# Layer 0's first modulation in four column chunks, the q projection summed with them, and q ahead of k/v for the later tiles

## The chip, the cores and the metric

The kernel runs on one core of one Trainium2 chip. A core has a matrix engine (TensorE; PE in the profile, its weight loads as PEld), a vector engine (VectorE, DVE), a scalar engine (ScalarE, ACT), GpSimd (POOL) and a sync engine (SP) that issues most transfers; 16 DMA engines move data between the chip's memory and the core's working memory. The metric is the device time of one execution in microseconds, the median of several runs.

## The reference

The reference is a diffusion backbone of two layers over 1024 latent tokens of width 1024 with a prefix of 256 context tokens. Only the entry of layer 0 matters here. From the condition vectors `c` (latent) and `c_ctx` (context) a modulation is computed, and tokens are scaled and shifted by its first two sixths; then one matrix gives the heads of two kinds of attention:

```python
m_lat = silu(c) @ ada_w[l] + ada_b[l]        # 6 x 1024 columns; m_ctx likewise from c_ctx
h_lat = x * (1 + m_lat[1]) + m_lat[0]        # h_ctx likewise
qa, ka, va, qb, kb, vb = split(h @ w_in, [512, 640, 768, 1280, 1792])   # 2304 columns
qa, ka = rms_norm(qa, q_gain), rms_norm(ka, k_gain)    # per head of 64 columns
qa, ka = apply_rope(qa, cos, sin), apply_rope(ka, cos, sin)   # latent tokens only
```

Attention, output projection, normalisation and a gated convolutional feed-forward follow, then layer 1. The other four sixths of `m_lat` and `m_ctx` are needed later.

## The kernel before, in words

Tokens are handled in ten tiles of 128: tiles 0 to 7 are latent, 8 and 9 are context. The function `l0_project` computes layer 0's projections. Products are made in three parts (`mm3`, L401 to L403): activations and weights are split into a high and a low half, and hi x hi, hi x lo and lo x hi are summed in PSUM, over eight blocks of 128 rows. A weight piece of 512 KB is loaded into a buffer of the ring `raw` (L125), and its halves are made by ACT (L112) and VectorE (L113).

The stages stand in this order on PE:

1. The head. `ada_first` loads the first 2048 columns of `ada_w[0]` as 16 tiles `wt` of 128 x 1024 (rows of 4 KB, L183) and multiplies `silu` of both condition vectors with them (L185). When all 16 are summed, four turns (L197) and a few small VectorE operations give the whole first modulation `mod0`. Meanwhile the rope table `rp`, then x of tiles 0 to 3 in two halves of 512 columns come in (L506).
2. `group(i, k)` turns one block of 128 columns of a group of four tiles (i = 0, 1; two context tiles for i = 2) on PE (L533), scales and shifts it on ACT into `sg` (L535) and makes the halves `hh` and `hl` (L542 to L545). Eight such groups of tiles 0 to 3 end the head. POOL makes the rope tables `tbq` and `tbk` from `rp` and the gains `gq` and `gk` (L555 to L563); VectorE scales `gq` first (L551).
3. k/v of tiles 0 to 3 (256 columns, weights `wk`), each with two groups of tiles 4 to 7 behind it; q of tiles 0 to 3 (512 columns, weights `wq`), each with two groups of the context behind it.
4. The generator `ada_items` is opened. It computes the other four sixths of layer 0's modulation on VectorE: loads `araw`, then `acc` sums (L231, L235), their halves (L322), a sum over partitions on PE (L325, L326), the bias (L330). Each `bg(n)` in the program takes up to n of its steps.
5. k/v of tiles 4 to 9 (with `bg(2)` at 8 and 9); q of tiles 4 to 9 with `bg(3)` each; v of the second attention, tiles 0 to 9 (weights `wv`), with `bg(3)` each. Behind v of tile 0 stand four turns (L145) with copies by VectorE (L147, `cc`) that bring the convolution's weights into columns.

A finished q or k tile is evacuated by `rms_rope`: ACT squares it (L584), VectorE sums per head (L586, `ss`) and makes the rotation's two products `rp` (L436, L446; for context tiles one product, L599), POOL makes the norm's factor (L589, L592), adds the products (L450) and scales (L605). `put_T` then turns the tile on PE (L471) and VectorE makes the low half `qst` (L459). This last part is put into the list `late` and runs three tiles later (`tok`).

Under `manual_pe` PE executes in the order in which the code is written; the order of the other engines is set by the framework's scheduler. Each engine executes its row strictly in order. Buffers come from pools with a fixed number of them: an allocation waits until the oldest buffer's readers are done. SP issues loads in order too, so a load that waits for its buffer holds up those behind it.

Of the kernel before, what the change touches and what calls it, by code (L numbers as in the profile page):

```python
# [12 lines left out]
ALU = mybir.AluOpType  # L13
# [24 lines left out]
class Kern:  # L38
# [93 lines left out]
    def cols_late(self, tp, ppool, rows, tag, pool=None, bufs=1):  # L132
# [10 lines left out]
        def make():  # L143
            ps = self.t(ppool, [128, 512], "small")
            nc.tensor.transpose(ps[:, :n], rt[:n, :], self.ident[:n, :n])  # L145
            ct = self.t(pool or self.cst, [128, n], tag)
            nc.vector.tensor_copy(ct, ps[:, :n])  # L147
            return ct
# [3 lines left out]
    def cols(self, tp, ppool, rows, tag, pool=None, bufs=1):  # L152
        return self.cols_late(tp, ppool, rows, tag, pool, bufs)()
# [8 lines left out]
    def ada_first(self, loads):  # L162

        nc, io = self.nc, self.io
        with ExitStack() as es:
            tp = es.enter_context(self.pool("p0"))
            ap = es.enter_context(self.pool("p0a"))
            wp = es.enter_context(self.pool("p0w", bufs=9))
            pp = es.enter_context(self.pool("p0s", bufs=1, space=PSUM))
            bias = self.row128(io["ada_b"][0, 0:2048])  # L170
            ct = self.cols(tp, pp, [io["c8"], io["cc8"], bias], "ccol")
            self.cs = self.t(self.cst, [128, 2, 8], "cs")
            nc.scalar.activation(
                self.cs, ct[:, :16].rearrange("p (v k) -> p v k", v=2), AF.Silu
            )
            w = io["ada_w"][0].rearrange("(k p) n -> p k n", p=128)
            ps = [self.t(pp, [128, 512], f"a{h}") for h in range(2)]
            for x in ps:
                nc.vector.memset(x[:, :256], 0.0)
            for k in range(KT):  # L180
                for h in range(2):
                    wt = self.t(wp, [128, 1024], "wt")
                    nc.sync.dma_start(wt, w[:, k, h * 1024 : (h + 1) * 1024])  # L183
                    for c in range(4):
                        nc.tensor.matmul(  # L185
                            ps[h][32 * c : 32 * c + 2, :256], self.cs[:, :, k],
                            wt[:, c * 256 : (c + 1) * 256], start=k == 0, stop=k == KT - 1,
                            tile_position=(0, 32 * c), skip_group_check=True,
                        )
            loads()  # L190
            ar = self.t(ap, [128, 2, 256], "ar")
            nc.scalar.copy(ar[:, 0], ps[0][:, :256])
            nc.vector.tensor_copy(ar[:, 1], ps[1][:, :256])
            pt = self.t(pp, [128, 512], "small")
            for j in range(4):
                s = slice(j % 2 * 128, j % 2 * 128 + 128)
                nc.tensor.transpose(  # L197
                    pt[:, j * 128 : (j + 1) * 128], ar[:, j // 2, s], self.ident
                )
            m0 = self.t(self.cst, [128, 2, 8, 2], "mod0")  # L200
            for h in range(2):
                nc.vector.tensor_add(
                    m0[:, h].rearrange("p (c b) v -> p c b v", b=2),
                    pt[:, h * 256 : (h + 1) * 256].rearrange(
                        "p (b c v) -> p c b v", b=2, c=4
                    )[:, :, :, :2],
                    ct[:, 16 + 8 * h : 24 + 8 * h].rearrange(
# [276 lines left out]
    def l0_project(self):  # L484
# [28 lines left out]
        with self.manual_pe():  # L513
            self.ada_first(first_loads)
# [2415 lines left out]
```

## Time and profile before

| | us |
|---|---|
| median of 3 runs (2925.42 to 2927.96) | 2925.8 |
| the profiled execution | 2927.96 |
| its span | 2926.1 |
| head, up to the first k/v product | 43.85 |
| first k/v product to the second v tile | 117.3 |
| the mean granted clock of TensorE over the span | 0.976 |

The busy time of an engine as a share of the span is an average over stages that have different limits. For this change the first 161 us count: a row of the windows view gives, for a stretch of the span, each engine's busy time, the clock that TensorE was granted (1.00 is full speed), the busy share of the DMA engines and the rate. A row of the timeline or of the chain of waits gives start, duration, engine, line and what is written from what; in the timeline, brackets hold the idle time before it and what ended that.

### The profile page before, as it was taken

What the parts mean: (1) busy time and instruction counts of PE and PEld (TensorE: products, weight loads), DVE (VectorE), ACT (ScalarE), POOL (GpSimd) and SP (SyncE); (2) the same over time, 40 slices, a digit from 0 to 9 for tenths busy, and PEclk for the clock granted to TensorE, in tenths of its full rate; (3) what the DMA queues carried; (4) which work ended last, traced back from release to release, by engine and by line L of the source; (5) the groups of instructions that cost most, each with busy time, mean ns of one, the idle gap of its engine ahead of it and who ended that gap; (6) DMA issues with size and microseconds to landing.
All of it is one profiled execution on the core that took longest, in us unless ns stands there. A gap on an engine that the chain in (4) does not pass through costs nothing.

```text
span 2926.1 us, 45178 instructions
## 1 busy us (share of the span) xinstructions
PE 2765.7 (95%) x16596; PEld 2254.8 (77%) x16596; DVE 2117.6 (72%) x3832; ACT 1383.0 (47%) x2597; POOL 691.5 (24%) x967
## 2 busy tenths in 40 slices
PE   6989999899999999999999987989998899999997
PEld 4877777777788988888888876866677688887886
DVE  4876366667588778888877656557766788888778
ACT  3221255567435655555553342257753545555541
POOL 2611143354451000000001013435544011111002
PEclk8999999999999999999999998989999999999999
DMA  8468711032567653333367526732244455555862
GB/s 261 141 188 275 229 39 41 11 128 94 160 161 241 207 169 107 119 107 114 117 236 272 163 83 195 226 106 64 65 132 146 126 172 164 176 171 201 325 219 93
DMA packets 370502, 456.87 MB, mean 156 GB/s; under 512 B 26137, under 2 KB 265017, under 8 KB 368745
## 3 DMA queue, kind: packets, MB, share of 16 engines
q1 hardware_dynamic: 342808, 369.40, 40.7%
q0 software_dynamic: 24576, 82.89, 8.2%
q8 instruction: 130, 2.13, 0.3%
q10 hardware_dynamic: 2896, 1.70, 0.2%
q14 instruction: 92, 0.75, 0.1%
HBM read 337.98 MB, written 115.93 MB: 155 GB/s over the span
## 4 chain that ended last, share of the span: by engine, by line
PE 68%; issue 10%; DVE 9%; DMA 6%; ACT 5%; POOL 1%; SPq 0%; ACTq 0%; DVEq 0%; POOLq 0%
PE q L1691 8%; PE x L1691 8%; PE y L1691 7%; PE S L762 4%; PE v L1691 4%; PE pv L907 3%; PE T L893 3%; PE dy L2354 3%; PE mm L401 2%; PE d L402 2%; PE d L403 2%; PE d L401 2%; PE mm L402 2%; PE mm L403 2%; PE dx L2354 2%
## 5 line engine op out<-in xcount | busy, mean ns | idle before, releaser
L786 POOL TENSOR_SCALAR P<-P,rin 128x640 f32<-128x640 f32 (+3 forms) x288 | 250.2, 873 | 347.3 <-DVE rin L785 324.0
L1665 DVE TENSOR_TENSOR w<-raw,w 128x512 fp32r<-128x512 f32 x308 | 207.3, 687 | 84.2 <-ACT w L1663 84.1
L112 ACT CAST w<-raw 128x512 fp32r<-128x512 f32 x315 | 183.3, 620 | 171.3 <-PE d L403 60.9
L113 DVE TENSOR_TENSOR w<-raw,w 128x512 fp32r<-128x512 f32 x299 | 194.2, 690 | 70.3 <-ACT w L112 68.2
L762 PE MATMUL S<-k,q 64*128 64x256 f32 (+2 forms) x1824 | 192.4, 338 | 16.9 <-DVE nm L2643 8.1
L783 ACT ACTIVATE P<-P,nm 128x641 f32<-128x641 f32 (+4 forms) x208 | 161.3, 777 | 83.0 <-DVE nm L2643 47.8
L1663 ACT CAST w<-raw 128x512 fp32r<-128x512 f32 x308 | 182.2, 621 | 13.8 <-DVE raw L1670 7.4
L762 PEld LDWEIGHTS S<-k,q 64*128 64x128 f32 x1824 | 136.1, 189 | 52.6 <-issue 17.8
L773 ACT COPY PT<-T 128x512 f32<-128x512 f32 (+1 forms) x250 | 134.0, 565 | 78.9 <-PE T L893 76.7
L907 PE MATMUL pv<-PT,v 128*64 128x128 f32 x2016 | 134.1, 281 | 16.3 <-ACT PT L773 14.1
L893 PE MATMUL T<-ident,P 128*128 128x128 f32 x1008 | 137.2, 283 | 7.9 <-POOL P L786 3.4
L907 PEld LDWEIGHTS pv<-PT,v 128*64 128x64 f32 x2016 | 109.5, 138 | 42.4 <-ACT PT L773 23.0
L401 PE MATMUL d<-w,w 128*128 128x512 f32 x352 | 138.0, 392 | 0.0
L403 PE MATMUL d<-w,w 128*128 128x512 f32 x352 | 137.7, 391 | 0.0
L402 PE MATMUL d<-w,w 128*128 128x512 f32 x352 | 137.6, 391 | 0.0
L785 DVE RECIPROCAL rin<-den 128x1 f32<-128x1 f32 x288 | 46.2, 162 | 121.0 <-ACT P L783 118.1
L893 PEld LDWEIGHTS T<-ident,P 128*128 128x128 f32 x1008 | 111.0, 143 | 28.5 <-issue 14.6
L771 DVE COPY PT<-T 128x512 f32<-128x512 f32 (+1 forms) x166 | 110.4, 666 | 30.7 <-PE T L893 20.6
L1691 PE MATMUL q<-T2h,w 128*128 128x512 f32 x352 | 117.7, 396 | 5.5 <-ACT q L1906 3.9
L1691 PE MATMUL q<-T3h,w 128*128 128x512 f32 x352 | 118.3, 397 | 4.0 <-DVE ug L2309 3.9
L2354 PE MATMUL dy<-w,w 128*128 128x512 f32 x528 | 120.8, 390 | 0.6 <-DVE w L113 0.6
L2643 DVE CUSTOM_DVE_ANT_0 P<-S,msk,snk 128x640 f32<-128x640 f32 (+1 forms) x128 | 103.7, 846 | 16.9 <-PE S L762 13.5
(417 smaller groups left out, 7802.2 us busy)
## 6 DMA issues: line engine op xcount, KB each, us to landing
raw<-in_up_dram SPq DMA_DIRECT2D x132, 512.0 KB
raw<-in_down_dram SPq DMA_DIRECT2D x59, 512.0 KB
raw<-g SPq DMA_DIRECT2D x44, 512.0 KB
raw<-G SPq DMA_DIRECT2D x38, 512.0 KB
araw<-in_ada_w_dram SPq DMA_DIRECT2D x32, 512.0 KB
raw<-in_w_in_dram SPq DMA_DIRECT2D x28, 512.0 KB
g<-cv POOLq DMA_DIRECT2D x22, 512.0 KB, 3.0
G<-go POOLq DMA_DIRECT2D x44, 256.0 KB, 2.7
```

What stands on the lines that cost most here:

```text
L112: nc.scalar.copy(hi, s)
L113: (lo_eng or nc.vector).tensor_sub(lo, s, f32(hi))
L401: nc.tensor.matmul(ps, lh, rh, start=first, stop=False)
L402: nc.tensor.matmul(ps, lh, rl, start=False, stop=False)
L403: nc.tensor.matmul(ps, ll, rh, start=False, stop=last)
L762: self.nc.tensor.matmul(outs[a], q[r, x, qs], k[r, y, ks], start=(i == 0), stop=(i == 2))
L786: nc.gpsimd.tensor_scalar(P[:, :n], P[:, :n], rin, 1.0, ALU.mult, ALU.mult)
L893: nc.tensor.transpose(ps[:, s * 128 : (s + 1) * 128], P[a][:, cols[i + x] : cols[i + x] + 128], self.ident,)
L907: nc.tensor.matmul(O[a * HD : (a + 1) * HD], v_of(a, vts[i + x]), pT[:, s * 128 : (s + 1) * 128], start=(i + x == 0), stop=(i + x == m - 1 ...
L1665: nc.vector.tensor_sub(half(i, 1), src[i], f32(half(i, 0)))
L1691: nc.tensor.matmul(ps, w[:, a, s], r[b][:, k], start=first and k + i == 0, stop=k == 3 and i == 2, skip_group_check=True,)
L2354: nc.tensor.matmul(banks[q][t], ga[i][:, a, c], wd[i][:, b], start=q < 2 and f + k == 0, stop=f == HF - 1 and k == 2, skip_group_check=True,)
```

## The change

The head is computed in four chunks j of columns. For each, four loads of 128 x 4 x 256 (pieces of 1 KB) bring the columns of shift and scale for two blocks k = 2j, 2j+1; `products(j, q)` multiplies half of a chunk (128 columns at a time), `turn_mod(j)` makes the two blocks' modulation, `turns(j)` turns the blocks of x, and `scaled` makes their halves. wq is loaded in four pieces of two blocks (`load_q`, `split_q`), and `part(j, t)` sums two of the eight blocks of q for tile t in a PSUM bank that is kept for each of tiles 0 to 3. So the sums of q begin when the first chunk is there. In this stretch the order is written by hand for PE, VectorE and ACT.

x is loaded in whole rows, in four buffers of 1024 columns in place of eight of 512. The rope table, gq, gk, wk and x of tiles 4 to 7 are loaded behind the head. Then q of tiles 0 to 3 is finished, k/v of tiles 0 to 3 follows with the groups of tiles 4 to 7, then q of tiles 4 to 9 with the context's groups, then k/v of tiles 4 to 9. `ada_items` is opened behind q of tile 7; `bg(3)` stands at q of tiles 8 and 9, `bg(2)` at k/v of tiles 4 to 9. `done` runs a waiting late part before it adds a new one.

```diff
-    def ada_first(self, loads):
+    def ada_first(self, tp, wp, pt, acc, m0):
...
+        def load(j):
+            for q in range(2):
+                for h in range(2):
+                    wt[j, q, h] = x = self.t(wp, [128, 4, 256], "wt")
+                    c0 = h * 1024 + j * 256
+                    nc.sync.dma_start(x, w[:, 4 * q : 4 * q + 4, c0 : c0 + 256])
+
+        def products(j, q):
+            s = slice(j % 2 * 128, j % 2 * 128 + 128)
+            for k in range(4 * q, 4 * q + 4):
+                for c in range(4):
+                    nc.tensor.matmul(
+                        acc[32 * c : 32 * c + 2, s], self.cs[:, :, k],
+                        wt[j, q, c // 2][:, k % 4, c % 2 * 128 : c % 2 * 128 + 128],
+                        start=k == 0, stop=k == KT - 1,
...
+            if q == 1:
+                ar[j] = self.t(tp, [128, 128], "ar", bufs=2)
+                nc.scalar.copy(ar[j], acc[:, s])
+
+        def turn(j):
+            ps = self.t(pt, [128, 4, 128], "tr")[:, 0]
+            nc.tensor.transpose(ps, ar[j], self.ident)
+            nc.vector.tensor_add(
+                m0[:, :, 2 * j : 2 * j + 2],
...
-        xp = ex.enter_context(self.pool("xp", bufs=8, side="right"))
+        xp = ex.enter_context(self.pool("xp", bufs=4, side="right"))
...
+        def load_q(j):
+            raws[j] = r = self.t(self.raw, [128, 2, 512], "raw")
...
+        def part(j, *ts):
+
+            for t in ts:
+                if j == 0:
+                    psq.append(self.t(pp, [128, 512], "mm"))
+                hi, lo, o = hT(t)
+                for k in (2 * j, 2 * j + 1):
+                    self.mm3(
+                        psq[t], hi[:, k, o : o + 128], lo[:, k, o : o + 128],
+                        *wq[k], k == 0, k == KT - 1,
+                    )
+
+        E = mybir.EngineType
+        engines = {E.PE, E.DVE, E.Activation}
+        with self.tc.manual_schedule(engines=engines), ExitStack() as e0:
...
+            def mod(j):
+                turn_mod(j)
+                for k in (2 * j, 2 * j + 1):
+                    scaled(0, k, trs.pop(k))
+
+            load_x(0)
+            load(0)
+            turns(0)
+            products(0, 0)
+            products(0, 1)
+            load_q(0)
+            load(1)
+            products(1, 0)
+            mod(0)
+            split_q(0)
+            load_q(1)
+            load(2)
+            products(1, 1)
+            part(0, 0, 1)
+            turns(1)
+            mod(1)
+            split_q(1)
+            part(0, 2, 3)
...
+            products(3, 0)
+            part(2, 0)
+            products(3, 1)
+            part(2, 1)
+            turns(3)
+            mod(3)
+            load_q(3)
+            split_q(3)
+            part(2, 2, 3)
...
+        def done(t, ps, ev):
             if len(late) > 3:
                 (late.pop(0) or int)()
+            late.append(ev(t, ps))
...
         with self.manual_pe():
-            load_x(1, 0)
-            load_x(1, 1)
-            wq = self.load_in(w, 0, 512)
+            load_x(1)
+            for t in range(4):
+                part(3, t)
+                done(t, psq[t], ev_qa)
             for t in range(4):
                 tok(t, wk, 256, ev_kva)
                 group(1, 2 * t)
                 group(1, 2 * t + 1)
-            load_x(2, 0)
-            load_x(2, 1)
-            for t in range(4):
+            load_x(2)
+            for t in range(4, NT):
                 tok(t, wq, 512, ev_qa)
-                group(2, 2 * t)
-                group(2, 2 * t + 1)
-            ex.close()
-            adap = es.enter_context(self.pool("adap", side="right"))
...
+                if t < 8:
+                    group(2, 2 * t - 8)
+                    group(2, 2 * t - 7)
+                if t == 7:
+                    ex.close()
+                    adap = es.enter_context(self.pool("adap", side="right"))
+                    ada = [
...
+                if t > 7:
+                    bg(3)
+            wv = self.load_in(w, 1792, 512)
             for t in range(4, NT):
                 tok(t, wk, 256, ev_kva)
-                if t > 7:
-                    bg(2)
-            wv = self.load_in(w, 1792, 512)
-            for t in range(4, NT):
-                tok(t, wq, 512, ev_qa)
-                bg(3)
+                bg(2)
```

In the rows that follow, a line number of the changed kernel is that of its own code (its `scaled` has L531 and L532 for the halves, its `rms_rope` L656 and L669, its rotation L432 and L442, `qst` L455, `acc` L227 and L231).

SP issues the loads. Before, at the end of x of tiles 0 to 3 (`x_254`, its last half row):

```order
L506 DMA x_254<-in_x_dram 128x1x512
L159 DMA gq_279<-in_qg_dram 128x64
L159 DMA gk_280<-in_kg_dram 128x64
L125 DMA raw_367<-in_w_in_dram 128x4x256
L125 DMA raw_375<-in_w_in_dram 128x4x256
L506 DMA x_394<-in_x_dram 128x1x512
```

After, from wq's last piece (`raw_494`) on; `raw_528` and `raw_536` are the two pieces of wk:

```order
L546 DMA raw_494<-in_w_in_dram 128x2x512
L620 DMA rp_114<-in_rope_dram 128x1024
L125 DMA raw_528<-in_w_in_dram 128x4x256
L159 DMA gq_524<-in_qg_dram 128x64
L159 DMA gk_525<-in_kg_dram 128x64
L501 DMA x_555<-in_x_dram 128x1x1024
L501 DMA x_557<-in_x_dram 128x1x1024
L501 DMA x_559<-in_x_dram 128x1x1024
L125 DMA raw_536<-in_w_in_dram 128x4x256
L501 DMA x_561<-in_x_dram 128x1x1024
```

The rope table, the gains and wk have moved behind the modulation's and q's weights, and x of tiles 4 to 7 comes in four whole tiles around wk's second piece.

VectorE in the head, before, from the end of `mod0` on:

```order
L211 TENSOR_SCALAR mod_79_264<-mod_79_264 128x16
L544 CAST hh_35_105<-sg_299 128x512
L545 TENSOR_TENSOR hl_36_106<-sg_299,hh_35_105 128x512
L544 CAST hh_35_105<-sg_317 128x512
L545 TENSOR_TENSOR hl_36_106<-sg_317,hh_35_105 128x512
L545 TENSOR_TENSOR hl_36_106<-sg_308,hh_35_105 128x512
L551 TENSOR_SCALAR gq_279<-gq_279 128x64
L544 CAST hh_35_105<-sg_335 128x512
```

After, at the last chunk (`mod_46_124<-tr_483` is its modulation, `sg_486` and `sg_490` its two blocks, `raw_494` wq's last piece):

```order
L113 TENSOR_TENSOR w_409<-raw_332,w_409 128x512
L113 TENSOR_TENSOR w_412<-raw_332,w_412 128x512
L625 TENSOR_SCALAR gq_524<-gq_524 128x64
L201 TENSOR_TENSOR mod_46_124<-tr_483,ccol_140 128x2x4
L531 CAST hh_35_105<-sg_486 128x512
L532 TENSOR_TENSOR hl_36_106<-sg_486,hh_35_105 128x512
L532 TENSOR_TENSOR hl_36_106<-sg_490,hh_35_105 128x512
L113 TENSOR_TENSOR w_496<-raw_494,w_496 128x512
L113 TENSOR_TENSOR w_499<-raw_494,w_499 128x512
```

The scaling of gq now stands ahead of the last chunk's modulation and halves.

VectorE where the modulation items begin, before (`mm_956` and `mm_1008` are k/v of tiles 4 and 5):

```order
L586 TENSOR_REDUCE ss_986<-sq_984 128x2
L436 TENSOR_TENSOR rp_239_991<-mm_956,tbk_388 128x128
L446 TENSOR_TENSOR rp_240_992<-mm_956,tbk_388 128x4x16 x2
L459 TENSOR_TENSOR qst_1003<-tr_998,qst_1003 128x512
L586 TENSOR_REDUCE ss_1038<-sq_1036 128x2
L436 TENSOR_TENSOR rp_248_1043<-mm_1008,tbk_388 128x128
L446 TENSOR_TENSOR rp_249_1044<-mm_1008,tbk_388 128x4x16 x2
L459 TENSOR_TENSOR qst_1055<-tr_1050,qst_1055 128x512
L231 TENSOR_SCALAR acc_277_1205<-araw_1207,cs_137 128x512
L231 TENSOR_SCALAR acc_278_1206<-araw_1207,cs_137 128x512
```

After (`mm_1107` is q of tile 7, `mm_1183` q of tile 8):

```order
L455 TENSOR_TENSOR qst_1134<-tr_1132,qst_1134 128x128
L432 TENSOR_TENSOR rp_246_1146<-mm_1107,tbq_545 128x512
L442 TENSOR_TENSOR rp_247_1147<-mm_1107,tbq_545 128x16x16 x2
L531 CAST hh_39_109<-sg_1156 128x256
L532 TENSOR_TENSOR hl_40_110<-sg_1163,hh_39_109 128x256
L532 TENSOR_TENSOR hl_40_110<-sg_1156,hh_39_109 128x256
L656 TENSOR_REDUCE ss_1220<-sq_1218 128x8
L455 TENSOR_TENSOR qst_1213<-tr_1208,qst_1213 128x512
L669 TENSOR_TENSOR q_1224<-mm_1183,gq_524 128x512
L227 TENSOR_SCALAR acc_263_1227<-araw_1229,cs_142 128x512
L227 TENSOR_SCALAR acc_264_1228<-araw_1229,cs_142 128x512
```

The first `acc` stood behind the evacuation of k/v of tile 5 and stands now behind that of q of tile 8, with the rotations of q of tiles 4 to 7 ahead of it.

More of the change, by code (lines that the diff above doesn't have):

```diff
@@ L129, in load_in, with cols_late @@
         return out
-    def cols_late(self, tp, ppool, rows, tag, pool=None, bufs=1):
+    def cols_late(self, tp, ppool, rows, tag, pool=None, bufs=1, bank="small"):
         nc = self.nc
@@ L143, in make @@
         def make():
-            ps = self.t(ppool, [128, 512], "small")
+            ps = self.t(ppool, [128, 512], bank)
             nc.tensor.transpose(ps[:, :n], rt[:n, :], self.ident[:n, :n])
@@ L159, in bcast @@
         self.nc.sync.dma_start(tile_ap, row.partition_broadcast(128))
-    def ada_first(self, loads):
+    def ada_first(self, tp, wp, pt, acc, m0):
         nc, io = self.nc, self.io
[L165 to L174, printed above, removed]
-            )
[L176 to L207, printed above, removed]
-                        "p (c b) -> p c b", b=2
-                    ).unsqueeze(3).to_broadcast([128, 4, 2, 2]),
-                )
-            nc.vector.tensor_scalar(m0[:, 1], m0[:, 1], 1.0, None, ALU.add)
-            self.mod0 = m0
@@ L545, in group, with hT @@
             nc.vector.tensor_sub(lo, sg[:, :n], f32(hi))
-        with self.manual_pe():
-            for k in range(KT):
-                group(0, k)
+        def group(i, k):
+            scaled(i, k, turn(i, k))
+        def hT(t):
+            c = H[t // 4]
+            return c[0], c[1], (t % 4) * 128
+        wq, psq, trs, raws = [], [], {}, {}
+        def load_q(j):
+            raws[j] = r = self.t(self.raw, [128, 2, 512], "raw")
+            wv = w.rearrange("(k p) n -> p k n", p=128)
+            nc.sync.dma_start(r, wv[:, 2 * j : 2 * j + 2, :512])
@@ new lines, in l0_project @@
+        E = mybir.EngineType
+        engines = {E.PE, E.DVE, E.Activation}
+        with self.tc.manual_schedule(engines=engines), ExitStack() as e0:
+            tp = e0.enter_context(self.pool("p0"))
+            wp = e0.enter_context(self.pool("p0w", bufs=9))
+            acc = self.t(pa, [128, 512], "small")
+            load, products, turn_mod = self.ada_first(tp, wp, pt, acc, m0)
+            def mod(j):
+                turn_mod(j)
+                for k in (2 * j, 2 * j + 1):
+                    scaled(0, k, trs.pop(k))
[17 more added lines that the diff above has]
+            part(0, 2, 3)
+            load_q(2)
+            load(3)
+            products(2, 0)
+            products(2, 1)
+            part(1, 0, 1)
+            turns(2)
+            mod(2)
+            split_q(2)
+            part(1, 2, 3)
+            products(3, 0)
[7 more added lines that the diff above has]
+            part(2, 2, 3)
```

88 lines of the change are left out of this document (51 added, 37 removed).

## The prediction

> **What bounds the kernel now.** I read the page first, then the stages of layer 0's projection, since all that the change moves lies there.
>
> ```profile
> span 2926.1 us, 45178 instructions
> PE 2765.7 (95%) x16596; PEld 2254.8 (77%) x16596; DVE 2117.6 (72%) x3832; ACT 1383.0 (47%) x2597; POOL 691.5 (24%) x967
> ```
>
> PE at 95% invites counting matmuls. The view of the engines' busy time by windows, cut at the kernel's stages, says where the rest is:
>
> ```profile
> core 0: us, PE busy (x) PEld busy (x) DVE busy (x) ACT busy (x) POOL busy (x), PEclk, DMA share, GB/s
> 0.00:43.85 43.85, 22.28 (x165) 8.06 (x165) 9.87 (x21) 9.87 (x16) 6.00 (x11) 0.78 0.96 313
> 43.85:64.10 20.25, 17.99 (x130) 17.70 (x131) 16.44 (x33) 13.10 (x27) 8.71 (x14) 0.81 0.63 184
> 64.10:88.20 24.10, 24.10 (x118) 19.95 (x117) 13.73 (x36) 9.72 (x24) 15.52 (x16) 1.00 0.28 85
> 109.60:150.40 40.80, 40.05 (x181) 32.17 (x180) 40.25 (x62) 9.63 (x20) 23.98 (x23) 1.00 0.50 151
> 150.40:161.10 10.70, 3.02 (x11) 1.82 (x10) 10.14 (x20) 3.24 (x6) 6.78 (x3) 0.67 0.74 213
> 161.10:219.50 58.40, 58.40 (x255) 48.05 (x254) 38.12 (x59) 11.34 (x20) 0.00 (x0) 0.97 0.57 178
> ```
>
> The stages are: the head (modulation and first transposes); kv of tiles 0 to 3; q of tiles 0 to 3; then, after kv of tiles 4 to 9 (88.20 to 109.60), q of tiles 4 to 9 with the first v tile; a stall; and v of tiles 1 to 9. Two holes stand out. In the head PE is busy 22.28 of 43.85 us while DMA is at 0.96. And from 150.40 PE does 3.02 us of work in 10.70. The waits between 120 and 165 us name the second, and the timeline gives the place:
>
> ```profile
> PE small L145 <- DVE cc L147: 4.8, 3, 3.4
> 96.66 1.01 DVE L231 TENSOR_SCALAR acc<-araw,cs 128x512 f32<-128x512 f32 x2
> 161.14 0.63 PE L401 MATMUL mm<-w,hh 128*128 128x512 f32 x1
> ```
>
> PE waits for the convolution's column copies (`cc`), which stand late in VectorE's row, and VectorE is busy 40.25 + 10.14 = 50.4 of the 51.5 us up to there: 98%. This full stretch begins at 96.66 with the first `acc` of the modulation carried along by `bg`, and ends where the second v tile starts on PE, at 161.14: a tail of 64.5 us. That tail, not PE, sets the end of the stage. Its groups:
>
> ```profile
> L235 DVE SCALAR_TENSOR_TENSOR acc<-araw,cs,acc 128x512 f32<-128x512 f32 x35 | 30.1, 889 | 2.6 <-DMA araw<-in_ada_w_dram 2.3
> L113 DVE TENSOR_TENSOR w<-raw,w 128x512 fp32r<-128x512 f32 x11 | 7.3, 701 | 0.0
> L459 DVE TENSOR_TENSOR qst<-tr,qst 128x512 fp32r<-128x512 f32 (+1 forms) x12 | 5.7, 478 | 0.0
> L586 DVE TENSOR_REDUCE ss<-sq 128x8 f32<-128x512 f32 (+1 forms) x10 | 5.2, 516 | 0.0
> L446 DVE TENSOR_TENSOR rp<-mm,tbq 128x256 f32<-128x256 f32 x8 | 3.0, 412 | 0.0
> L436 DVE TENSOR_TENSOR rp<-mm,tbq 128x512 f32<-128x512 f32 x4 | 2.7, 678 | 0.0
> L599 DVE TENSOR_TENSOR q<-mm,gq 128x512 f32<-128x512 f32 x2 | 1.4, 682 | 0.0
> ```
>
> So the question is when the first `acc` can run in the changed kernel, and how long the tail is then.
>
> **The change part by part.** I follow PE from the head to the first `acc`, then VectorE through the tail. From the second v tile on both kernels have the same order, so I cost the rest at nothing. One thing is carried over: `bg` is called 48 times up to the end of v instead of 52, and four of its steps, some 4 us of VectorE each at most, run later; beside v VectorE is busy 38.12 of 58.40 us and PE is full, so that covers them, and without that cover they would add to VectorE's tail of the next stage.
>
> *The chunked head, up to q of tiles 0 to 3 done.*
>
> ```profile
> 1.88 13.34 SPq L183 DMA_DIRECT2D wt<-in_ada_w_dram  x16
> 6.01 1.04 PE L185 MATMUL a<-wt,cs 128*2 128x256 f32 x8 [2.41 <-DMA wt<-in_ada_w_dram]
> 11.05 0.61 PE L185 MATMUL a<-wt,cs 128*2 128x256 f32 x8 [0.25 <-DMA wt<-in_ada_w_dram]
> DMA packets 894, 3.27 MB, mean 409 GB/s; under 512 B 98, under 2 KB 98, under 8 KB 893
> DMA packets 1288, 1.17 MB, mean 292 GB/s; under 512 B 324, under 2 KB 1175, under 8 KB 1288
> DMA packets 909, 1.50 MB, mean 250 GB/s; under 512 B 90, under 2 KB 263, under 8 KB 909
> ```
>
> The three DMA lines are the windows 17 to 25 (rows of 4 KB), 33 to 37 (mostly k/v's weights in pieces of 1 KB) and 37 to 43 (half rows of x, 2 KB). The new modulation loads come in pieces of 1 KB, so I take 292 GB/s for them and 409 for x, now whole rows. Data flow from about 4.7 us (first issue 1.88, landed 6.01). PE reaches the first summing, `part(0)`, behind x (2.1 MB, 5.1 us), two chunks and one piece of wq (4.7 MB, 16.1 us) and the last products: about 27.5. The last chunk has landed by about 44.
>
> The prices on PE, from the chain of waits in order of time:
>
> ```profile
> 51.92 0.87 PE tr L533 x8
> 52.79 0.12 PE mm L401
> 64.14 0.23 PE mm L401
> 69.71 0.44 PE tr L533 x4
> 161.34 0.43 PE mm L401
> ```
>
> From 27.5 PE has `part` 0 to 2 for four tiles, 12 times 6 matmuls at 0.23 = 16.6; five half chunks of products, each the work of two old tiles, 2 x 0.61 = 1.2, together 6.1; three pairs of turned tiles at 0.87 plus a turned modulation, 0.11 each, 2.9. (0.11 is a quarter of the 0.44.) That ends at 53, behind the data, so PE carries this stretch. Then the last chunk's hi/lo halves. VectorE has gq's scaling (L625) ahead of the last modulation's sum, and gq's load waits until the chunk buffers, whose space it takes, are given up (behind it on SP stand gk, x of tiles 4 to 7 and the second piece of k/v's weights); beside the halves POOL builds the rope tables:
>
> ```profile
> 34.83 0.43 DVE L544 CAST hh<-sg 128x512 fp32r<-128x512 f32 x1 [5.06 <-ACT sg L535]
> 35.29 0.69 DVE L545 TENSOR_TENSOR hl<-sg,hh 128x512 fp32r<-128x512 f32 x1
> 38.53 1.27 POOL L555 TENSOR_TENSOR tbq<-rp,gq 128x512 f32<-128x512 f32 x1 [37.23 <-PE tr L533]
> 38.78 1.30 DVE L544 CAST hh<-sg 128x512 fp32r<-128x512 f32 x1 [0.39 <-ACT sg L535]
> 40.12 2.23 DVE L545 TENSOR_TENSOR hl<-sg,hh 128x512 fp32r<-128x512 f32 x2
> 43.44 2.04 POOL L563 TENSOR_TENSOR tbk<-rp,gk 128x256 f32<-128x256 f32 x2
> ```
>
> Ahead of the tables a half took 0.43 and 0.69, beside them 1.30 and 1.1. I add 1.5 us (between 0 and 5), nearest to one stretched pair. `part(3)`, 4 x 1.38 = 5.5, ends at 60. Its bounds: 53 if data and halves never hold PE up, 65 if the loads run at 250 GB/s or the halves wait out the tables.
>
> *From there to the first `acc`.* Before, the modulation items were opened ahead of kv of tiles 4 to 9; now they are opened behind q of tile 7 and first run behind q of tile 8. PE has kv of tiles 0 to 3, each 24 x 0.12 + 0.87 (turning x) + 0.44 (the late turning of a q tile) = 4.2, together 16.8; q of tiles 4 to 7 with the context turned, 24.1 as in the window; q of tile 8, a quarter of that, 6.0; and its evacuation:
>
> ```profile
> 70.34 0.69 DVE L586 TENSOR_REDUCE ss<-sq 128x8 f32<-128x512 f32 x1 [1.55 <-ACT sq L584]
> 71.54 0.74 DVE L446 TENSOR_TENSOR rp<-mm,tbq 128x256 f32<-128x256 f32 x2
> 71.11 0.20 POOL L589 TENSOR_SCALAR ss<-ss 128x8 f32<-128x8 f32 x1 [2.06 <-DVE ss L586]
> 74.57 1.04 POOL L605 TENSOR_TENSOR q<-q,ss 128x512 f32<-128x512 f32 x1
> ```
>
> 2.2 from the end of its products (69.71 in this example) to the last read. Together 49.1.
>
> Three waits are new on this way. k/v's second weight buffer comes free only when wq's last piece is split: 1 us. The context's loads wait for buffers that the turning of tiles 4 to 7 gives up, and a load takes 4.1 us from issue to landing by the first row above; behind a late load stand q of tile 4's turnings and all of PE: 2 us (0 to 4). POOL's part of a q tile is 4.5 us (71.11 to 75.61), and four of them come 1.4 us apart: the turned q of tile 0 is then late for kv: 1 us (0 to 4). Sum 4. First `acc` at 60 + 49.1 + 4 = 113.1, against 96.66.
>
> *The tail.* Counted in VectorE's row from the first `acc` to the last `cc`: `acc` sums 37 instead of 35 (+1.8); weight halves 9 for 11 (-1.4); `qst` 8 for 12, five wide ones as before (-1.5); `ss` 7 for 10, wide ones 1 for 6 (-2.8); the rotations of four q tiles gone (-5.7), those of two k tiles more in it (+1.4, a quarter of their width); gq's products 1 for 2 (-0.7). Sum -8.9; the groups overlap a little, so -8.5: 64.5 becomes 56. Low end 51 (the 2.6 us of idle time go, and POOL, 23.98 us busy beside it before, gets out of the way), high end 60 (a wait for one more load).
>
> *Sum.* Second v tile at 113.1 + 56 = 169.1 against 161.1: +8. The profiled execution took 2927.96 us (span 2926.1), 2.2 above the median of 2925.8. At the median: 2934. What a measurement tells from no change, 0.2%, is 5.9 us. The break-even is q of tiles 0 to 3 done at 52.
>
> What the change saves is real, but on PE: 12 of the 16 parts, 16.6 us, move under the loads. They buy PE a lead that it then spends at the `cc` copies.
>
> **The rivals.**
>
> *PE decides after all: faster.* The 16.6 us reach the end: 2909. For it: PE at 95%, and the head's hole of 21.6 us. Against it: the 98% of VectorE. It holds only if the first `acc` runs by 161.1 - 16.6 - 56 = 88.5, that is, if q of tiles 0 to 3 is done by 35, before the last chunk has landed; a milder form, done at 53, no new waits, a tail of 51, gives 153 and 2918. Chance 0.10.
>
> *The loads lose nothing by their pieces: no change.* At 409 GB/s for the chunks `part(0)` starts 4.6 us sooner, q ends at 55.5, and the sum is +3.4: 2929. For it: the window at 292 GB/s also held 324 small packets of the broadcast rows, which may be what slowed it. Against it: 2 KB rows ran at 250. The Trainium skill, "DMA: Bandwidth & Descriptors", Specifications, puts the least transfer for full rate at 512 B, by which 1 KB pieces cost nothing; the 250 GB/s of 2 KB rows do not agree. Chance 0.23.
>
> *The tables hold the last chunk: slower still.* If each half waits for whole POOL instructions, the four halves wait out the 6.95 us of tables (38.53 to 45.48), 5 beyond my 1.5 less: q ends at 65, +13: 2939. For it: 0.43 became 1.30, as long as the POOL row beside it. Against it: halves did pass between the tables' rows. The Trainium skill, "SBUF — State Buffer", Who interferes with whom, has it that VectorE and GpSimd share a port pair as an exclusive lock, held for a whole instruction; the 1.30 agrees. Chance 0.12.
>
> *A cold clock.* The granted clock was 0.78 and 0.81 in the first two stages, and a matmul behind the stall took 0.43 instead of 0.23. If the parts run so, 16 x 6 x 0.20 = 19 us of loss, 14 on the path (2 to 5 hidden by loads): q ends at 74, +22: 2948. Against it: at 52.79, 9 us behind the head, a matmul of 256 columns took 0.12, and now more work stands there to keep PE going. Chance 0.07.
>
> **How the numbers follow.** The forecast, +8, has 0.48. Range 2922 to 2948: from the tail's low end with q done at 53 (53 + 49.1 + 4 + 51 = 157.1, -4) to the cold clock; left out are the first rival and half of the last. Its own range is 2930 to 2940. Faster by over 0.2%: 0.10, the first rival. Within: the second, 0.23, and the forecast's low edge, 0.05: 0.28. Slower: the rest, 0.62.
>
> **What the profile after would show.** First `acc` near 113 and second v tile near 169 (each within 4), with VectorE at about 98% between; last chunk landed near 44; first matmul of kv tile 0 near 60; POOL's tables and stretched halves at 50 to 58; a wait of PE for the context ahead of q of tile 4; a stall at the `cc` copies not shorter than 10.7. All stages from the second v tile on last as long as before. I am wrong if VectorE has gaps in that tail, if the first `acc` comes before 105, or if the difference arises after the second v tile.

## The result, and the profile after

The changed kernel is slower: 2942.43 us in the median (2934.93 to 2945.91) against 2925.8 us before, a ratio of 1.0042 with a 95% interval of 1.003 to 1.0055, or 12 us (9 to 16). The two medians lie 16.6 us apart, and the changed kernel's own runs spread over 11 us, so the size of the loss is known to a few microseconds only. The forecast was 2934.

The page of the profiled execution (2942.43 us, span 2940.7) has nearly the same work as before:

```profile
span 2940.7 us, 45393 instructions
PE 2775.5 (94%) x16724; PEld 2264.3 (77%) x16724; DVE 2112.5 (72%) x3832; ACT 1386.2 (47%) x2600; POOL 690.4 (23%) x967
```

The view by windows is cut at the new stages: up to the first q product; the parts of q of tiles 0 to 3; k/v of tiles 0 to 3; q of tiles 4 to 9 as far as the first `acc`; the rest of q with k/v of tiles 4 to 9 and the first v tile; the column copies; the other v tiles.

```profile
core 0: us, PE busy (x) PEld busy (x) DVE busy (x) ACT busy (x) POOL busy (x), PEclk, DMA share, GB/s
0.00:29.18 29.18, 12.88 (x138) 6.19 (x138) 2.90 (x10) 4.40 (x8) 0.69 (x6) 1.00 0.94 273
29.18:63.95 34.77, 32.34 (x251) 24.71 (x252) 18.34 (x30) 13.24 (x24) 9.52 (x9) 1.00 0.82 240
63.95:84.04 20.09, 17.39 (x146) 16.70 (x144) 16.03 (x36) 11.38 (x26) 18.86 (x21) 1.00 0.50 142
84.04:119.22 35.18, 32.87 (x157) 26.84 (x156) 19.95 (x45) 12.78 (x27) 25.19 (x31) 1.00 0.33 103
119.22:167.00 47.78, 34.64 (x211) 31.01 (x211) 44.68 (x85) 14.30 (x34) 23.02 (x27) 0.82 0.74 216
167.00:172.58 5.58, 2.45 (x8) 1.47 (x7) 4.26 (x11) 1.06 (x3) 0.00 (x0) 0.72 0.68 207
172.58:230.00 57.42, 57.42 (x247) 47.08 (x246) 35.52 (x56) 10.97 (x21) 0.00 (x0) 0.97 0.49 151
```

The head's hole has become smaller: before, PE did 22.3 us of work in the first 43.9; now it does 45.2 in the first 64. A new hole stands from 119.22 to 172.58, where PE is busy 37.1 of 53.4 us and VectorE 48.9. The waits of that stretch (119 to 173) say for what:

```profile
PE small L321 <- ACT ahl L317: 12.3, 2, 6.4
PE small L145 <- DVE cc L147: 2.6, 3, 1.5
```

The timeline gives the marks; its last row here is the first mask of layer 0's attention:

```profile
119.22 0.87 DVE L227 TENSOR_SCALAR acc<-araw,cs 128x512 f32<-128x512 f32 x2
172.58 0.63 PE L397 MATMUL mm<-w,hh 128*128 128x512 f32 x1
363.38 0.42 DVE L1062 TENSOR_SCALAR_CACHE_REDUCE P<-S 128x256 f32<-128x256 f32 x1 [0.41 <-PE S L834]
```

and the same operation in the timeline before:

```profile
350.69 0.42 DVE L990 TENSOR_SCALAR_CACHE_REDUCE P<-S 128x256 f32<-128x256 f32 x1 [0.40 <-PE S L762]
```

`ahl` are the halves of a finished `acc`. PE meets the modulation's partition sums (L321) in its row before VectorE has made what they read, and waits there 12.3 us. The first `acc` is 22.6 us later than before, the second v tile 11.4 us (172.58 against 161.14), the attention 12.7 us. All of the loss stands ahead of the second v tile but for 1.3 us.

### The profile page after: what moved, and what is told of

Same layout as the page of the kernel before. It is cut to its first block, busy times and chain, and to the rows that moved or that the text cites. A ratio compares the mean times of both kernels' runs of the same rounds, so it can differ in the third digit from the quotient of the medians.

```text
span 2940.7 us, 45393 instructions
## 1 busy us (share of the span) xinstructions
PE 2775.5 (94%) x16724; PEld 2264.3 (77%) x16724; DVE 2112.5 (72%) x3832; ACT 1386.2 (47%) x2600; POOL 690.4 (23%) x967
## 4 chain that ended last, share of the span: by engine, by line
PE 66%; issue 10%; DVE 10%; DMA 7%; ACT 5%; POOL 2%; SPq 1%; ACTq 0%; POOLq 0%; DVEq 0%
PE q L1763 7%; PE x L1763 7%; PE y L1763 7%; PE S L834 4%; PE pv L979 3%; PE v L1763 3%; PE T L965 3%; PE dy L2426 3%; PE d L397 3%; PE d L398 3%; PE d L399 3%; PE mm L397 2%; PE mm L398 2%; PE mm L399 2%; PE dx L2426 2%
## 5 line engine op out<-in xcount | busy, mean ns | idle before, releaser
L2426 PEld LDWEIGHTS dy<-w,w 128*128 128x128 f32 x528 | 98.9, 188 | 21.8 <-DVE w L113 0.8
```

The source lines that it names most:

```text
L2426: nc.tensor.matmul(banks[q][t], ga[i][:, a, c], wd[i][:, b], start=q < 2 and f + k == 0, stop=f == HF - 1 and k == 2, skip_group_check=True,)
```

## The experiments

The marks of all kernels are taken from the timelines of their profiled executions (us), one for each; the ratio is that of the timed runs to the kernel before, with its interval. Runs of one kernel lay up to 17 us apart (before_cc8: 2910.66 to 2927.51), and an execution that was profiled can be the slowest of its kernel (kt_123: 2925.08, where the median is 2914.18), so 3 us at a mark alone are an indication. The second v tile is marked by its first product. The steps are those that `bg` is asked for ahead of the second v tile.

| kernel | first k/v product | first `acc` | second v tile | attention | steps | ratio |
|---|---|---|---|---|---|---|
| before | 43.85 | 96.66 | 161.14 | 350.69 | 25 | 1 |
| changed | 63.95 | 119.22 | 172.58 | 363.38 | 21 | 1.0042 (1.003 to 1.0055) |
| order_only | 82.41 | 128.19 | 179.87 | 366.85 | 21 | 1.0055 (1.0041 to 1.0068) |
| kvfirst | 65.98 | 111.45 | 167.47 | 356.93 | 25 | 1.0016 (1.0008 to 1.0025) |
| after_bk1 | 64.61 | 118.05 | 162.59 | 352.65 | 15 | 1.0002 (0.9993 to 1.001) |
| tab8 | 60.14 | 116.59 | 169.97 | 355.47 | 21 | 1.0018 (1.0008 to 1.0027) |
| ctx_early | 64.27 | 115.45 | 169.02 | 357.82 | 21 | 1.0028 (1.0016 to 1.0039) |
| before_cc8 | 43.19 | 96.33 | 153.07 | 345.10 | 25 | 0.998 (0.9968 to 0.9992) |
| kt_123 | 62.17 | 108.93 | 156.58 | 340.30 | 17 | 0.9961 (0.9947 to 0.9974) |
| early_kv13 | 60.33 | 96.62 | 156.63 | 339.03 | 27 | 0.997 (0.9959 to 0.9982) |
| before_k1q2 | 43.29 | 97.17 | 153.59 | 343.56 | 17 | 0.9967 (0.9957 to 0.9978) |
| early_kv12_cc8 | 60.46 | 96.12 | 147.75 | 338.27 | 21 | 0.9952 (0.9937 to 0.9967) |

The theory: VectorE's row from the first `acc` to the column copies sets the end of this stage. The rivals: PE's own work and the head set it, or what is put off only comes back later.

**order_only.** The old head, and only the new order behind it.

```diff
             wq = self.load_in(w, 0, 512)
             for t in range(4):
+                tok(t, wq, 512, ev_qa)
+                group(1, 2 * t)
+                group(1, 2 * t + 1)
+            load_x(2, 0)
+            load_x(2, 1)
+            for t in range(4):
                 tok(t, wk, 256, ev_kva)
...
```

> The head of the kernel before, and only the changed order behind it: q of tiles 0 to 3 with the groups of tiles 4 to 7, k/v of tiles 0 to 3, q of tiles 4 to 9 with the context, then k/v, bg as in the changed kernel. Theory (VectorE's tail): q done at 43.9 + 4 x 6.6 = 70, first acc at 70 + 13 + 24 + 6 + 2 + 4 = 119 to 126, second v tile at 173 to 180: 12 to 20 us slower than before, at or above the changed kernel; what the chunked head is worth is the difference of the two, 0 to 8. Rival (the head's 16.6 us on PE reach the end, and something in the new head costs them back): as the kernel before, within 3 us.

The order alone costs 16 us (12 to 20), and the rival's 3 us are excluded; the first `acc` came 2 us behind its range, the second v tile within it. In its windows, VectorE is busy 48.84 of the 51.68 us between first `acc` and second v tile and PE 36.57:

```profile
128.19:179.87 51.68, 36.57 (x215) 31.81 (x215) 48.84 (x95) 15.24 (x36) 22.80 (x27) 0.83 0.72 216
```

Against it, the changed kernel shows what the chunked head is worth: 18.5 us at the first k/v product (3.5 of them the groups of tiles 4 to 7, which it still has to turn), 9.0 at the first `acc`, 7.3 at the second v tile, 3.5 at the attention. In the timed runs the two intervals overlap.

**kvfirst.** The chunked head with k/v ahead of q for tiles 4 to 9.

```diff
             load_x(2)
-            for t in range(4, NT):
-                tok(t, wq, 512, ev_qa)
+            for t in range(4, 8):
+                tok(t, wk, 256, ev_kva)
+                group(2, 2 * t - 8)
+                group(2, 2 * t - 7)
...
+            for t in (8, 9):
+                tok(t, wk, 256, ev_kva)
+                bg(2)
+            wv = self.load_in(w, 1792, 512)
+            for t in range(4, NT):
+                tok(t, wq, 512, ev_qa)
+                bg(3)
```

> The chunked head is kept; for tiles 4 to 9 k/v stands ahead of q again, the context's groups stand at k/v of tiles 4 to 7, and the modulation items open behind k/v of tile 7. Theory (VectorE's tail sets the stage, so its first acc does): first acc at 84 + 4 x 3.4 + 3 (context's wait) + 2.9 + 1.5 = 105 instead of 119.2, the tail about 62 as in the kernel before, second v tile at 166 to 168 instead of 172.6; 4 to 6 us faster than the changed kernel, still 5 to 8 slower than before. Rival (PE's work and the head decide; the order is neutral): as the changed kernel, within 2 us.

First `acc` at 111.45, 6 us later than expected but 7.8 sooner than in the changed kernel; the second v tile where it was expected, because two misses met: the tail was 56 us and not 62. The time is 1.0016, its interval apart from that of 1.0042. The work is the same, the first `acc` stands earlier, and about 60% of the loss went.

**after_bk1.** Fewer modulation steps at k/v.

```diff
             for t in range(4, NT):
                 tok(t, wk, 256, ev_kva)
-                bg(2)
+                bg(1)
```

> The changed kernel with bg(1) for bg(2) at k/v of tiles 4 to 9: six steps of the modulation items, of 3 to 3.5 us of VectorE each, leave the tail for later. Theory (VectorE's tail): PE's wait of 12.3 us for the halves of acc goes, second v tile 14 to 18 us sooner (155 to 159), and VectorE has the room for the six steps beside v, where it was busy 35.5 of 57.4 us; 7 to 14 us faster than the changed kernel at the end. Rival (PE and the head decide): within 2 us of the changed kernel. Rival (the work only comes back): second v tile sooner, but the same end.

One of PE's two waits for `ahl` is gone, the other is as long as in the changed kernel (waits from 118 to 164):

```profile
PE small L321 <- ACT ahl L317: 6.4, 1, 6.4
PE small L145 <- DVE cc L147: 4.3, 3, 3.5
```

So the second v tile came 10.0 us sooner, not 14 to 18; but all of that, 10.7 us, is still there at the attention, and the time is that of the kernel before. Beside v VectorE had the room. The two rivals fall.

**tab8.** The rope tables made ahead of the last chunk.

```diff
+            nc.sync.dma_start(rp, io["rope0"])
+            self.bcast(gq, io["qg"][0])
+            self.bcast(gk, io["kg"][0])
             part(0, 0, 1)
...
             split_q(2)
+            nc.vector.tensor_scalar(gq, gq, HD ** -0.5, None, ALU.mult)
+            tabs = {}
...
             part(1, 2, 3)
```

> The changed kernel with the rope table, gq and gk loaded behind the third chunk and POOL's tables made ahead of the last chunk (eight chunk buffers instead of nine give the space). Theory (the tables hold up the last chunk's halves and weights, 4 us of q's end at 64, and then POOL's q tiles): q of tiles 0 to 3 done at 59 to 60, first acc 4 to 7 us sooner (112 to 115), second v tile at 166 to 168; 4 to 7 us faster than the changed kernel. Rival (the lateness of q is the loads' and PE's): q's end stays at 63 to 64, no change; or the tables now stretch the third chunk's halves and PE waits there instead.

The first k/v product came 3.8 us sooner, as expected. What the tables had held up shows in VectorE's timeline: four low halves of weights, which stand between the last chunk and `part(3)`. In the changed kernel:

```profile
56.30 4.63 DVE L113 TENSOR_TENSOR w<-raw,w 128x512 fp32r<-128x512 f32 x4
```

In tab8:

```profile
54.07 2.49 DVE L113 TENSOR_TENSOR w<-raw,w 128x512 fp32r<-128x512 f32 x4
```

How the 3.8 us split differs between executions. Behind the turn of the last chunk's modulation (52.33 us in the changed kernel, 50.81 in tab8) lie 2.3 of them. The other 1.5 lie in `part(0)`: in the changed kernel several of its first matmuls came 0.43 us apart and not 0.23, though the granted clock is given as 1.00 there. In after_bk1 and ctx_early, which have the changed kernel's head, these came 0.23 apart, but PE waited as long in `part(3)` and some of the matmuls behind that wait came slowly, and the mark is as late (64.61 and 64.27). The four kernels with the tables late have it at 63.95 to 65.98, the four with them early at 60.14 to 62.17, so the size stands; why matmuls come slowly at a clock of 1.00 is not shown.

2.6 us of it were left at the first `acc` and at the second v tile, less than expected there; but 7.9 at the attention and 7 us in the time (1.0018 for 1.0042). The 5 us that came behind the second v tile are for the most part waits of PE for loads (`raw`, pieces of `ada_w` for layer 1's modulation, which PE sums into `cols`) and slower matmuls. From there to the attention, first in the changed kernel, then in tab8:

```profile
PE cols L301 <- DMA raw<-in_ada_w_dram: 4.7, 2, 2.4
172.58:363.38 190.80, 184.39 (x965) 145.96 (x965) 98.92 (x168) 32.82 (x61) 16.09 (x32) 0.97 0.70 219
PE cols L301 <- DMA raw<-in_ada_w_dram: 3.0, 1, 3.0
169.97:355.47 185.50, 181.46 (x965) 144.07 (x965) 99.47 (x168) 32.78 (x61) 16.23 (x32) 0.99 0.72 225
```

The same 965 matmuls kept PE busy 2.9 us less, at a granted clock of 0.99 and not 0.97, and 1.7 us of that wait went. Why these loads came in time in one kernel and not in the other no run here shows.

**ctx_early.** The context loaded ahead of time.

```diff
-                x[i, j] = r = self.t(xp, [128, D], "x")
+                x[i, j] = r = (
+                    self.t(self.raw, [128, D], "raw") if i == 2 else self.t(xp, [128, D], "x")
+                )
...
             load_x(1)
+            load_x(2)
```

> The changed kernel with the context's two tiles loaded behind x of tiles 4 to 7 into two buffers of the weight ring, which are free there, instead of x buffers that the groups of tiles 4 to 7 give up. Theory (a wait of PE ahead of the first acc goes through to the end, since VectorE's tail starts so much sooner): PE's two waits for the context (2.3 us) go, first acc at 116 to 117 instead of 119.2, the attention 2 to 4 us sooner than 363.4 in the changed kernel. Rival (the wait hides another, for POOL's q tiles or the halves of tile 7): first acc within 1 us of 119.2.

```profile
115.45 0.88 DVE L227 TENSOR_SCALAR acc<-araw,cs 128x512 f32<-128x512 f32 x2
```

3.8 us at the first `acc`, 3.6 at the second v tile, 5.6 at the attention: a wait of PE ahead of the first `acc` goes through. 2.5 of the 3.8 lie where the context's waits were (PE has none there now); the rest came in k/v of tiles 0 to 3, which was not expected. The ratios' intervals overlap, so the time alone would not tell.

**before_cc8.** The kernel before, with the column copies (where its stall was) behind v of tile 8.

```diff
             for t in range(NT):
                 tok(t, wv, 512, ev_vb)
-                if t == 0:
+                if t == 8:
                     self.conv = [f() for f in conv]
```

> The kernel before with the convolution's four column turns and their cc copies behind v of tile 8 instead of tile 0. Theory (the cc copies only show VectorE's lateness; its row of acc sums is what is late): PE's stall of 10.7 us at the copies goes and the second v tile comes about 10 us sooner, but PE meets the modulation's sums instead, and the attention starts 0 to 4 us sooner than 350.7. Rival (the copies themselves are the bottleneck): the whole 8 to 10 us reach the attention and the end.

The second v tile came 8.1 us sooner and the attention 5.6, the time 0.998. That is between the two expectations. PE's waits from 120 to 206 us show smaller ones in place of the one of 10.7:

```profile
PE small L325 <- DVE abr L330: 3.4, 2, 2.5
PE small L145 <- DVE cc L147: 2.8, 3, 1.9
```

So the place of the copies is a cause of its own. That VectorE has had time to catch up behind v of tile 8 fits these waits, but was not tried by itself.

**kt_123 and early_kv13.** Both have the chunked head and the tables of tab8. kt_123 has the order of kvfirst with `bg(1)` at k/v of tiles 8 and 9 and `bg(2)` at q. early_kv13 loads the context as ctx_early does, turns it at k/v of tiles 0 to 3 and opens the modulation there:

```diff
             for t in range(4):
                 tok(t, wk, 256, ev_kva)
                 group(1, 2 * t)
                 group(1, 2 * t + 1)
+                group(2, 2 * t)
+                group(2, 2 * t + 1)
+            ex.close()
+            adap = es.enter_context(self.pool("adap", side="right"))
...
+            for t in range(4, NT):
+                tok(t, wk, 256, ev_kva)
+                bg(1)
+            wv = self.load_in(w, 1792, 512)
+            for t in range(4, NT):
+                tok(t, wq, 512, ev_qa)
+                bg(3)
```

> Chunked head, tables early (tab8), the order of the run kvfirst for tiles 4 to 9, and fewer modulation steps ahead of the second v tile: bg(1) at k/v of tiles 8 and 9, bg(2) at q of tiles 4 to 9, bg(3) at v; 17 steps instead of 25 in the kernel before. Theory (VectorE's tail, and it has room beside v): first acc at 106 to 109, second v tile at 153 to 158 instead of 161.1 in the kernel before, attention at 341 to 346 instead of 350.7: 5 to 10 us faster than before. Rival (the steps put off come back whole behind v): second v tile sooner, attention at 350 or later, no gain.

> Chunked head, tables early, the context loaded early and turned at k/v of tiles 0 to 3, so that the modulation items open before tile 4; then k/v of tiles 4 to 9 with bg(1), q of tiles 4 to 9 with bg(3). Theory (first acc decides): first acc at 92 to 96, as in the kernel before (96.7) or sooner; 27 steps against 25 ahead of the second v tile, which then comes at 154 to 160; attention at 338 to 345: 6 to 12 us faster than before. Here the lead that the chunked head gives PE can be spent, because VectorE starts as soon. Rival (the chunked head's own waits eat its lead): second v tile at 161 or later, no gain.

Both are faster than the kernel before, by 11 us (8 to 16) and 9 us (5 to 12). Two ways lead there: kt_123 starts the tail 12 us later than before and shortens it to 47.7 us; early_kv13 starts it as before and has 60.0. Of the gain at the attention, 10.4 and 11.7 us, only 4.6 and 4.5 stand at the second v tile. The rest comes behind it, where neither kernel has PE's wait for the loads of `cols`, which is 4.7 us in the kernel before.

**before_k1q2.** How much of kt_123 is the chunked head? The old head and order, with its steps.

```diff
                 if t > 7:
-                    bg(2)
+                    bg(1)
...
                 tok(t, wq, 512, ev_qa)
-                bg(3)
+                bg(2)
```

> The kernel before with the modulation steps of the run kt_123: bg(1) at k/v of tiles 8 and 9, bg(2) at q of tiles 4 to 9, bg(3) at v; 17 steps for 25 ahead of the second v tile, nothing else changed. Against kt_123 (0.9961) it tells what the chunked head gives when VectorE's tail doesn't bind. Theory (the head's lead on PE comes through once the tail is short): second v tile at 153 to 158, attention at 344 to 347, 3 to 6 us faster than before, and kt_123 still 5 to 8 us ahead of it. Rival (the head gives nothing; all of the gain of kt_123 is the steps put off): attention at 340, 0.996 as kt_123.

Two numbers in the old kernel make it 10 us faster (6 to 13). kt_123, with the chunked head, the early tables and kvfirst's order, is 3.0 us later at the second v tile and 3.3 sooner at the attention, and nothing that the time can tell (0.9961 and 0.9967). The time is that of the rival, the attention lies between the two expectations: nearly all of kt_123's gain can be had from the steps alone, and no lead of the head is left at the second v tile. The windows up to the column copies, of the copies and of the other v tiles show why the steps don't come back: VectorE is full ahead of the second v tile, and has 23 us of room beside v.

```profile
109.00:145.00 36.00, 36.00 (x167) 29.61 (x166) 35.72 (x58) 9.17 (x19) 27.29 (x23) 1.00 0.53 161
145.00:154.20 9.20, 4.24 (x21) 3.12 (x20) 9.20 (x18) 3.73 (x7) 3.11 (x3) 0.90 0.83 245
154.20:215.00 60.80, 60.80 (x263) 49.98 (x262) 37.79 (x59) 14.24 (x25) 1.06 (x2) 0.96 0.55 169
```

**early_kv12_cc8.** The best parts together: early_kv13 with `bg(2)` at q and the copies behind v of tile 8.

> The run early_kv13 with bg(2) for bg(3) at q of tiles 4 to 9 and the four column turns behind v of tile 8: modulation opened early, 21 steps ahead of the second v tile. Theory (what is left is PE's own work): second v tile near 151, attention at 336 to 340, within 3 us of early_kv13 and kt_123. Rival (VectorE still binds there): 3 us or more faster than both.

0.9952, 14 us (10 to 18) faster than the kernel before and the fastest here, though its interval overlaps those of kt_123 and early_kv13. By the ratios it is 3 and 5 us ahead of them, between the two expectations. From its first `acc` to the end of the copies PE is busy 97.98 of 101.88 us and VectorE 88.23: here little is left but PE's own work.

```profile
96.12:198.00 101.88, 97.98 (x473) 80.97 (x471) 88.23 (x153) 25.41 (x54) 41.20 (x36) 1.00 0.66 196
```

**x_plain.** A look at a term of the head: why x came slowly.

```diff
-                    nc.sync.dma_start(r, xs[4 * i + j])
+                    t = 4 * i + j
+                    nc.sync.dma_start(r, io["x"][t * 128 : (t + 1) * 128, :])
```

> The changed kernel with tiles 0 to 7 of x loaded as 128 neighbouring rows each instead of 16 groups of 8 rows, 64 rows (256 KB) apart; tokens then stand in another order, so the rest computes something else in the same time. In the changed kernel x of tiles 0 to 3 came at 235 GB/s (window 5 to 13), though in rows of 4 KB, and the modulation's 1 KB pieces at 355. Theory (the distance of the rows slows x, not the size of the pieces): x at 370 to 410 GB/s, the last of its first four tiles landed 3 to 4 us sooner, first q product at 25.5 to 27 instead of 29.2. Rival (x comes slowly because it is the first load, or by something else): 235 to 260 GB/s and 29.2 again.

The DMA of the changed kernel from 5 to 13 us, and from 14 to 29 us (mostly the modulation's pieces):

```profile
DMA packets 627, 1.88 MB, mean 235 GB/s; under 512 B 64, under 2 KB 204, under 8 KB 627
DMA packets 4841, 5.33 MB, mean 355 GB/s; under 512 B 168, under 2 KB 4328, under 8 KB 4840
```

That of x_plain from 5 to 10 us, and its first q product, which stood at 29.18 in the changed kernel:

```profile
DMA packets 905, 1.96 MB, mean 391 GB/s; under 512 B 55, under 2 KB 552, under 8 KB 905
...
25.07 0.51 PE L397 MATMUL mm<-w,hh 128*128 128x512 f32 x1 [1.04 <-ACT w L112]
```

With neighbouring rows x comes at 391 GB/s and the head's parts begin 4.1 us sooner, 0.4 us ahead of the range expected. The layout of the rows slows x, not the size of its pieces, which is 4 KB in both. In this one execution the first `acc` came at 115.94 and the attention at 359.85, 3.3 and 3.5 us sooner than in the changed kernel: a delay of the first load, too, goes through to the first `acc`.

## Why the prediction was right, and where it was off

**What sets the end.** The main step held: the new order moves the first `acc` back, VectorE's tail goes with it, and PE's lead from the head is spent waiting. order_only and kvfirst show the place of the first `acc` as the cause from both sides, ctx_early with a single edit, after_bk1 and before_k1q2 that VectorE's work ahead of the second v tile is what is waited for. The place of the wait was wrong: PE lost most at the modulation's sums (12.3 us), not at the column copies.

**q of tiles 0 to 3, 60 predicted, 63.95 measured.** Three terms were off: the first part began 1.7 us late; the parts with their products took 26.2 us and not 25.5, the slow matmuls of `part(0)` included; and the last chunk held PE up by 3.1 us, where 1.5 were put. The last is the step that was mis-sized. I looked at the halves of x alone, but the low halves of the weights stand behind them in VectorE's row, and POOL's tables hold up each subtraction. Rows of the timeline after, the last without a POOL instruction beside it:

```profile
57.46 1.18 POOL L637 TENSOR_TENSOR tbk<-rp,gk 128x256 f32<-128x256 f32 x1
57.97 1.22 DVE L113 TENSOR_TENSOR w<-raw,w 128x512 fp32r<-128x512 f32 x1
58.60 1.18 POOL L637 TENSOR_TENSOR tbk<-rp,gk 128x256 f32<-128x256 f32 x1
59.11 1.22 DVE L113 TENSOR_TENSOR w<-raw,w 128x512 fp32r<-128x512 f32 x1
60.25 0.68 DVE L113 TENSOR_TENSOR w<-raw,w 128x512 fp32r<-128x512 f32 x1
```

Each subtraction ended 0.55 us after the POOL row beside it (58.64 and 59.19, 59.78 and 60.33), and the two took turns. So did the two low halves of x and the first of the weights, which took 1.11, 1.21 and 1.75 us. The rival of the tables was therefore nearer than the forecast both in number (65) and in mechanism, waits for whole POOL instructions; but here only the five subtractions waited so, and `part(3)` could begin between them. The Trainium skill, "SBUF — State Buffer", Who interferes with whom, has the shared pair of ports held for a whole instruction; these rows agree. The load of gq, on which VectorE sat idle for 4.2 us, cost nothing: PE, without a wait, came to turn the last modulation only at 52.33, and gq's scaling had begun at 52.18.

The chain of waits after goes on from there (picked rows):

```profile
61.89 1.66 POOL ss L662
73.04 1.27 POOL q L446
77.81 1.27 POOL q L446
87.56 4.92 DMA x<-in_ctx_dram
92.52 0.55 PE tr L513 x3
```

That the first part began only 1.7 us late is partly luck: two terms ahead of it were wrong and met halfway. x came at 235 GB/s where I took 409 (3.8 us later), and the chunks at 347 to 355 where I took 292 (2.9 us sooner); the first part began at 29.2 for 27.5. On the pieces the truth lay between the forecast and the second rival (409), and the gain was lost to x. The Trainium skill, "DMA: Bandwidth & Descriptors", Why small descriptors are slow, counts three fixed cycles to a packet; by that a 1 KB piece would run at 382 GB/s (an estimate from its 32-byte beats and the 409 of the 4 KB rows), and the measured 355 lies a little below.

**k/v of tiles 0 to 3, 16.8 plus 2 predicted, 20.1 measured.** POOL was busy 18.86 of these 20.09 us, and stands in the chain with q's factors and products: four bunched q tiles at some 4.6 us each. I had the price and gave the wait 1 us; PE's waits came to 2.7 us here, 1.5 of them for the `qst` of a turned q tile. The context's wait, 2 us, was measured at 2.3, and ctx_early gives 3.8.

**The first `acc`, 113.1 predicted, 119.2 measured.** The sum of these misses: 4 from q, 1.3 from k/v, and the rest, 0.9, between there and the first `acc`.

**The tail, 56 predicted, 53.4 measured.** The counts were right to within one or two; the `acc` sums were shorter. First the changed kernel, with the first product of each sum in the second row, then that row before:

```profile
L231 DVE SCALAR_TENSOR_TENSOR acc<-araw,cs,acc 128x512 f32<-128x512 f32 x38 | 28.4, 800 | 2.3 <-DMA araw<-in_ada_w_dram 2.3
L227 DVE TENSOR_SCALAR acc<-araw,cs 128x512 f32<-128x512 f32 x6 | 2.9, 511 | 0.0
L231 DVE TENSOR_SCALAR acc<-araw,cs 128x512 f32<-128x512 f32 x6 | 4.8, 816 | 0.1
```

0.800 instead of 0.889 us, 38 times, is 3.4 us, and the first products give 1.9 more. The reason is the one that I had put into the low end, POOL out of the way: it was busy 23.0 of these 53.4 us and 41.2 of the 64.5 before, 6 of the 38 sums waited for a POOL instruction (11 of 35 before), and behind the second v tile of the kernel before, with POOL idle, a sum took 0.747. VectorE was busy 92% there and not 98%, with 4 us of gaps for loads (2.3) and for the high halves of weights that ACT makes (1.4). I had named gaps as a sign of being wrong: by them loads, and not VectorE's own work, set up to 4 us of this tail. The stall at the copies was not as long as before, as I had it, but 5.6 us: PE met VectorE's lateness sooner, at the modulation's sums.

**The sum.** +8 predicted at the second v tile, +11.4 measured, and 1.3 more up to the attention: the way to the first `acc` 6 us up, the tail 2.6 down. That the sum came within 4 us is partly luck, since the two misses have opposite signs.

**The rivals.** PE deciding fell with the 12.3 us at L321. Of the cold clock, which was to cost 14 us on the path, some 1.5 us of slow matmuls in `part(0)` showed; the granted clock was 1.00 in both stages up to 64 us.

## What to carry to other kernels

Work taken off the busiest engine buys nothing while another engine's row ends the stage: find the last wait of the stage, go back to where the work behind it could first start, and see whether the change moves that start. Here it moved it 22.6 us back, and two numbers that put off background work to a stage with room were worth more (10 us) than the whole rebuilt head (3 to 4 us at the attention, which the times can't tell from nothing). A generator of background steps is a load on the engine that does them: place its steps by that engine's room in each stage, and open it as soon as its buffers can be had.

## What the runs showed of the hardware that was not expected

- Loads of 4 KB rows ran at 235 GB/s when a tile took 16 groups of 8 rows, 256 KB apart, and at 391 GB/s with 128 neighbouring rows; pieces of 1 KB, in rows 24 KB apart, ran at 355. The Trainium skill, "DMA: Bandwidth & Descriptors", Latency and other measured facts, tells of a like loss for row distances of 512 KB and above (207 GB/s at 512 KB). Here a loss shows with 256 KB between groups; whether the distance or the grouping makes it was not tried.
- Beside POOL's table products, a subtraction on VectorE with two operands in the core's memory waited for the whole POOL instruction: it ended 0.55 us after it, and four in a row took 4.63 us instead of 2.49.
- At a granted clock of 1.00, several matmuls of `part(0)` came 0.43 us apart in one execution and 0.23 in others of the same head.
